# The column steps of two triangular inversions on GpSimd in place of VectorE, spread alike, with one more task step behind them

## The chip, the cores and the metric

The kernel runs on one core of one Trainium2 chip. The metric is the device time of that core in microseconds; the kernel before takes 983.41 us (median of 3 runs, 983.08 to 984.17). Engines are named as in the profile: PE is TensorE's matrix multiply, PEld its weight load, DVE is VectorE, ACT ScalarE, POOL GpSimd, SP SyncE. Each engine works off its own queue strictly in order; SP and POOL also issue the DMAs of their queues.

## The reference

One decoder block over 512 tokens of width 1024, in float32. A combined projection feeds two branches, a gated delta rule (8 heads, chunks of 64) and a forgetting attention (8 heads, causal softmax with a decay bias); they are merged by gates and followed by a squared-ReLU MLP. The part that the change touches is the triangular solve of the delta rule:

```
kk = jnp.einsum('bhncd,bhnsd->bhncs', k, k)
a_mat = jnp.where(tri_strict, beta[..., None] * kk * decay, 0.0)
rhs = jnp.concatenate([v * beta[..., None], k * (beta * jnp.exp(G))[..., None]], axis=-1)
sol = lax.linalg.triangular_solve(a_mat + eye, rhs, left_side=True, lower=True, unit_diagonal=True)
...
v_new = value_c - jnp.einsum('bhcd,bhde->bhce', kcum_c, s)
o = einsum(qdec_c, s) + einsum(attn_c, v_new);  s = s * dec_c + einsum(kdec_c, v_new)
...
m = sigmoid(gate_a) * y_a + sigmoid(gate_b) * y_b;  h = x + m @ w_out
x = h + jnp.square(jax.nn.relu(rmsnorm(h) @ w_up)) @ w_down
```

The kernel does not solve, it inverts the unit triangular matrices, here in blocks of 128 tokens, and multiplies by the inverse.

## The kernel before

**Stages.** The input is normalised and split into a rounded high part and a low rest; so is every weight (`hi` on ACT, line 256, and `lo` on DVE, line 257, a subtraction of two 128x1024 tiles in SBUF), and each product is three products on PE. First come the z gates and the projections of heads 0 to 3 (group 0), then six attention panels (`fox_pair`, products `fx`, lines 961 to 964), the projections of heads 4 to 7 (group 1), then the stream of 49 weight units (`stream`, products `st`, line 1011, 24 products each) for the rest of the attention heads and the gates, then the output projections and the MLP (`mlp`, line 1171), which holds PE from about 620 us to the end. Of every seven weight tiles of the stream four are not loaded but made from an earlier tile: POOL issues a DMA that adds onto the earlier raw tile (line 219), and it has to wait until that tile's `lo` was read out.

**Tasks.** Beside these loops run generator tasks, one per head, per inversion and scan, per attention worker. A call of `tick` advances each by one step, to its next `yield`. What a task writes between two yields is placed at that point of the program.

**What sets the order.** The program is written in that order, and a scheduler then rearranges each engine's queue by its own estimate of when each instruction is ready. So a change on one engine also moves rows of the others.

**The inversion** (`invert`, lines 659 to 747) runs once per group, over the 16 blocks of four heads at a time. The four 32x32 diagonal blocks of each are brought into one tile `E` (DVE transpose, line 669), and `X` starts as the identity. Then 31 columns are eliminated, two instructions each (lines 681 and 683): an outer product of a column of `E` with a row of `X` into `tmp`, and its subtraction from the rows below. The operands have r = 31 - j rows of n = j//2 + 1 elements per partition, 16 to 136 elements, 2,856 in all for each of the two lines. Each instruction reads what the one before it wrote. `INV_STEP` says after how much counted work the task yields. Behind the columns two DVE transposes make `Xd` (line 689) and its transpose `XT` (line 692), `X2` is filled (memset on POOL, copies on ACT), and PE joins the blocks by small products: `Qp` (line 707, needs `Xd`), `Tp` (line 720), `Q` and `T` (lines 739 and 741). After that `scan` goes over the four chunks.

**Around it on POOL**: scaling of queries and keys (`conv` line 652, `fqk` line 889), reciprocal roots by a power (`rsq`, line 346: `ssk`, `fss`, `sso`), the attention mask (`nd`, line 878), and the adding DMAs.

Of the kernel before, what the change touches and what calls it, by code (L numbers as in the profile page):

```python
# [10 lines left out]
ALU = mybir.AluOpType  # L11
# [4 lines left out]
P = 128  # L16
# [21 lines left out]
LA_NEW = 7  # L38
LA_RAW = 3
LA_SPLIT = 2  # L40
INV_STEP = (2500, 900)


def hybrid_block(tc, a, out):
# [21 lines left out]
    def nm(s):  # L66
        n_names[0] += 1
        return f"{s}_{n_names[0]}"
# [5 lines left out]
    def page(dt=F32, s="pg"):  # L74
        if s in FOX_TAGS:
            return fxp.tile([P, T], dt, tag=s, name=nm(s))
        tag = TAGS_OF.get(s, s)
        if tag in TAGS:
            return pgp.tile([P, T], dt, tag=tag, name=nm(s), bufs=TAGS[tag])
        return pgp.tile([P, T], dt, tag="pg", name=nm(s))  # L80
# [3 lines left out]
    def const(shape, s, dt=F32):  # L84
        return (cp if s in KEEP else cm).tile(shape, dt, tag=s, name=s)
# [15 lines left out]
    def atps(s="at"):  # L101
        return pat.tile([P, T], F32, tag="at", name=nm(s))

    def v3(ap, n):
        return ap.rearrange("p (a b) -> p a b", a=n)
# [8 lines left out]
    vec, act, pool = nc.vector, nc.scalar, nc.gpsimd  # L114
# [542 lines left out]
    x_id = const([P, B * HB], "x_id")  # L657

    def invert(AT, rest, ahead):

        bl = [slice(b * B, (b + 1) * B) for b in range(4)]
        dg = page(s="dg")
        for b in range(4):
            act.copy(v3(dg[bl[b], :], NI), AT[bl[b], :, bl[b]])
        yield
        E_ = sbp.tile([P, B * B], F32, tag="sub", name=nm("E"))
        vec.transpose(E_[:, :].rearrange("p (c d i) -> p c d i", c=B, d=2),
                      dg[:, :].rearrange("p (i c) -> p c i", i=NI).unsqueeze(2).to_broadcast([P, B, 2, NI]))  # L670
        X_ = page(s="X")
        vec.tensor_copy(X_, x_id)
        yield
        E3 = v3(E_[:, :], B)
        X3 = v3(X_[:, :], B)
        w = 0
        for j in range(B - 1):
            r, n = B - 1 - j, j // 2 + 1
            tmp = smp.tile([P, 144], F32, tag="tmp", name=nm("tmp"), bufs=2)
            t3 = tmp[:, 0:r * n].rearrange("p (a b) -> p a b", a=r)  # L680
            vec.tensor_tensor(t3, E3[:, j + 1:, j:j + 1].to_broadcast([P, r, n]),
                              X3[:, j:j + 1, 0:n].to_broadcast([P, r, n]), op=ALU.mult)
            vec.tensor_tensor(X3[:, j + 1:, 0:n], X3[:, j + 1:, 0:n], t3, op=ALU.subtract)
            w += 2 * (130 + r * n)
            if w > rest:
                w = 0
                yield
        Xd = page(s="Xd")
        vec.transpose(Xd[:, :].rearrange("p (i c d) -> p c d i", i=NI, d=2),
                      X_[:, :].rearrange("p (r c) -> p c r", c=HB))  # L690
        XT = page(s="XT")
        vec.transpose(XT, Xd)
        Xd3 = v3(Xd[:, :], NI)
        XT3 = v3(XT[:, :], NI)

        X2 = sbp.tile([P, NI, 64], F32, tag="sub", name=nm("X2"))
        pool.memset(X2[0:32, :, 32:64], 0.0)
        act.copy(X2[0:32, :, 0:32], Xd3[0:32, :, :])
        act.copy(X2[32:64, :, 32:64], Xd3[32:64, :, :])
        yield  # L700

        qs = page(s="Q")
        pqs = [atps("Qp") for _ in range(2)]
        for i in range(NI):
            for p in range(2):
                b0, b1 = bl[2 * p], bl[2 * p + 1]
                mm(pqs[p][b1, i * B:(i + 1) * B], AT[b0, i, b1], Xd3[b0, i, :], start=True, stop=True)
        for p in range(2):
            b1 = bl[2 * p + 1]
            (vec.tensor_copy if p else act.copy)(qs[b1, :], pqs[p][b1, :])  # L710
        for b in range(4):
            act.copy(AT[bl[b], :, bl[b]], XT3[bl[b], :, :])
        yield
        pqs = [atps("Tp") for _ in range(2)]
        pq = atps("Tq")
        for i in range(NI):
            s = slice(i * B, (i + 1) * B)
            for p in range(2):
                b0, b1 = bl[2 * p], bl[2 * p + 1]
                mm(pqs[p][b0, s], qs[b1, s], XT3[b1, i, :], start=True, stop=True)  # L720
                if p == 0:
                    mm(pq[b1, s], XT3[b1, i, :], qs[b1, s], start=True, stop=True)
        for p in range(2):
            b0, b1 = bl[2 * p], bl[2 * p + 1]
            act.mul(AT[b0, :, b1], v3(pqs[p][b0, :], NI), -1.0)
        vec.tensor_scalar(X2[bl[1], :, 0:32], v3(pq[bl[1], :], NI), -1.0, None, op0=ALU.mult)
        yield
        ahead()
        q6 = None
        for j0 in range(0, NI + 8, 8):  # L730
            last, more = q6, j0 < NI
            if last is not None:
                pt = atps("T6")
            if more:
                pq = atps("Q6")
            for i in range(8):
                s = slice(i * 64, (i + 1) * 64)
                if last is not None:
                    mm(pt[0:64, s], last[64:128, s], AT[64:128, j0 - 8 + i, 64:128], start=True, stop=True)
                if more:  # L740
                    mm(pq[64:128, s], AT[0:64, j0 + i, 64:128], X2[0:64, j0 + i, :], start=True, stop=True)
            if last is not None:
                act.mul(AT[0:64, j0 - 8:j0, 64:128], v3(pt[0:64, :], 8), -1.0)
            if more:
                q6 = page(s="Q6s")
                vec.tensor_copy(q6[64:128, :], pq[64:128, :])
            yield
# [4 lines left out]
    def fetch(g, hd, kind, c):  # L752

        t = page(s="hd")
        nc.sync.dma_start(v3(t[:, :], G), hd[kind, c])
        return [t[:, cs(i)] for i in range(G)]
# [74 lines left out]
    def group_chain(g, AT, hd, heads):  # L831
        while any(t in tasks for t in heads):
            yield
        got = []
        yield from invert(AT, INV_STEP[g], lambda: got.extend(fetch(g, hd, kind, 0) for kind in (3, 2, 4)))
        inverted[g] = True
        yield from scan(g, AT, hd, got)
# [385 lines left out]
    for n in range(KT):  # L1223
        s_, j, f = n // 4, n // 2 % 2, n % 2
# [165 lines left out]
    for k, (w, c, p, s_) in enumerate(MLP):  # L1390
# [6 lines left out]
        n = pos[0]  # L1397
# [122 lines left out]
```

## Time and profile before

| what | value |
|---|---|
| time, median of 3 runs | 983.41 us |
| span of the profiled execution | 980.2 us |
| granted PE clock | 1.000 |
| PE busy | 970.8 us (99%) |
| DVE busy | 710.9 us (73%) |
| ACT busy | 605.0 us (62%) |
| POOL busy | 240.2 us (25%) |
| column steps of group 0 on DVE | 143.49 to 170.44 us |
| column steps of group 1 on DVE | 354.41 to 400.06 us |
| first small product `Qp`, group 0 and 1 | 174.95 and 418.64 us |

Times within the trace count from the start of the span. A row of the timeline has the start, the duration, the engine, the line, the operation, what it writes and reads, the shapes, and the idle time before it with what ended it. "x4" merges four alike.

### The profile page before, as it was taken

The page shows a single profiled execution, that of the slowest core. Times are in us where ns is not written, and L with a number is a line of the kernel's source. Part 1 is how long each engine was busy: PE and PEld are TensorE (multiplying, and loading weights), DVE is VectorE, ACT ScalarE, POOL GpSimd, SP SyncE. Part 2 cuts the span into 40 slices and gives each one's busy share as a digit, 9 for nine tenths or more (in the row PEclk, how much of TensorE's full clock was granted, in tenths as well). Part 3 has the DMA queues.
Part 4 walks back from the last instruction along what each step waited for, and adds up shares of the span by engine and source line. Part 5 has one row for each costly group of instructions (what it writes and reads, how often), then busy time and mean ns, then how long its engine had stood idle before and what let it go on. Part 6 is the DMA issues. An engine that isn't in the chain of part 4 may idle for free.

```text
span 980.2 us, 17198 instructions
## 1 busy us (share of the span) xinstructions
PE 970.8 (99%) x6545; PEld 874.8 (89%) x6545; DVE 710.9 (73%) x1204; ACT 605.0 (62%) x1050; POOL 240.2 (25%) x236
## 2 busy tenths in 40 slices
PE   8999999999999999999999999999999999999998
PEld 6788899998888999999999888889989989988986
DVE  6877778566577789855656535889896697698596
ACT  7766444766564787867656422678755765666761
POOL 1544120202533513522320005312121121121110
PEclk9999999999999999999999999999999999999999
DMA  7647662475437885757887735688798888889884
GB/s 266 213 135 223 174 158 90 130 239 181 129 116 228 189 166 141 197 129 166 236 201 215 273 103 171 125 181 173 190 188 196 187 173 206 181 175 202 186 166 119
DMA packets 93442, 174.38 MB, mean 178 GB/s; under 512 B 8016, under 2 KB 49200, under 8 KB 93360
## 3 DMA queue, kind: packets, MB, share of 16 engines
q1 hardware_dynamic: 78928, 120.85, 38.8%
q0 software_dynamic: 14432, 52.44, 30.5%
q8 instruction: 51, 0.84, 0.4%
q14 instruction: 31, 0.25, 0.1%
HBM read 152.25 MB, written 21.02 MB: 177 GB/s over the span
## 4 chain that ended last, share of the span: by engine, by line
PE 92%; DVE 4%; DMA 2%; ACT 1%; issue 1%; SPq 0%; DVEq 0%
PE mlp L1171 36%; PE st L1011 12%; PE mm L279 8%; PE mm L276 8%; PE mm L275 8%; PE fx L964 2%; PE fx L961 2%; PE fx L962 2%; PE fo L944 2%; PE sc L919 1%; PE pT L935 1%; DVE lo L257 1%; PE kk L639 1%; PE kq L647 1%; DMA ux<-ud 1%; PE v L797 1%
## 5 line engine op out<-in xcount | busy, mean ns | idle before, releaser
L1402 ACT CAST hi<-draw 128x1024 fp32r<-128x1024 f32 x124 | 130.0, 1050 | 118.4 <-PE mlp L1171 100.4
L1409 DVE TENSOR_TENSOR lo<-draw,hi 128x1024 fp32r<-128x1024 f32 x124 | 151.3, 1222 | 44.8 <-ACT hi L1402 41.6
L256 ACT CAST hi<-raw 128x1024 fp32r<-128x1024 f32 (+1 forms) x62 | 62.9, 1021 | 82.6 <-PE mm L276 59.5
L1171 PE MATMUL mlp<-hi,shi 128*128 128x512 f32 x280 | 109.5, 391 | 0.1
L1171 PE MATMUL mlp<-hi,slo 128*128 128x512 f32 x280 | 109.1, 390 | 0.0
L1171 PE MATMUL mlp<-lo,shi 128*128 128x512 f32 x280 | 109.0, 389 | 0.0
L257 DVE TENSOR_TENSOR lo<-raw,hi 128x1024 fp32r<-128x1024 f32 (+1 forms) x62 | 73.9, 1197 | 29.1 <-ACT hi L256 13.4
L1171 PE MATMUL mlp<-shi,lo 128*128 128x256 f32 x448 | 90.3, 283 | 0.0
L1171 PE MATMUL mlp<-slo,hi 128*128 128x256 f32 x448 | 90.3, 283 | 0.0
L1171 PE MATMUL mlp<-shi,hi 128*128 128x256 f32 x448 | 90.3, 283 | 0.0
L276 PE MATMUL mm<-ulo,hi 128*128 128x512 f32 x216 | 85.0, 394 | 1.2 <-DVE ulo L290 1.2
L275 PE MATMUL mm<-uhi,hi 128*128 128x512 f32 x216 | 85.0, 395 | 0.0
L257 DVE TENSOR_TENSOR lo<-sraw,hi 128x1024 fp32r<-128x1024 f32 x49 | 60.7, 1240 | 20.9 <-ACT hi L256 20.1
L1171 PEld LDWEIGHTS mlp<-shi,hi 128*128 128x128 f32 x448 | 70.6, 192 | 0.9
L1171 PEld LDWEIGHTS mlp<-shi,lo 128*128 128x128 f32 x448 | 69.9, 192 | 0.0
L1171 PEld LDWEIGHTS mlp<-slo,hi 128*128 128x128 f32 x448 | 69.8, 192 | 0.0
L256 ACT CAST hi<-sraw 128x1024 fp32r<-128x1024 f32 x49 | 51.3, 1047 | 26.6 <-PE st L1011 16.2
L1171 PEld LDWEIGHTS mlp<-hi,shi 128*128 128x128 f32 x280 | 52.6, 188 | 11.1 <-issue 0.7
L1171 PEld LDWEIGHTS mlp<-lo,shi 128*128 128x128 f32 x280 | 52.6, 188 | 11.1
L1171 PEld LDWEIGHTS mlp<-hi,slo 128*128 128x128 f32 x280 | 52.6, 188 | 10.3
L219 POOL DMA_DIRECT2D draw<-w_d x30 | 26.3, 876 | 129.9 <-DVE lo L1409 120.8
L219 POOL DMA_DIRECT2D draw<-w_u x32 | 27.7, 866 | 122.6 <-DVE lo L1409 120.0
(336 smaller groups left out, 2466.6 us busy)
## 6 DMA issues: line engine op xcount, KB each, us to landing
draw<-w_u POOLq DMA_DIRECT2D x32, 512.0 KB, 5.7
draw<-w_d POOLq DMA_DIRECT2D x32, 512.0 KB, 6.5
sraw<-w_st POOLq DMA_DIRECT2D x28, 512.0 KB, 5.9
draw<-w_d SPq DMA_DIRECT2D x26, 512.0 KB, 4.4
raw<-w_gdn SPq DMA_DIRECT2D x24, 512.0 KB, 3.8
draw<-w_u SPq DMA_DIRECT2D x24, 512.0 KB, 4.4
sraw<-w_st SPq DMA_DIRECT2D x21, 512.0 KB, 5.5
hd<-hd SPq DMA_DIRECT2D x34, 256.0 KB, 5.4
```

What stands on the lines that cost most here:

```text
L219: nc.gpsimd.dma_start(raw, a[w][c, q, s_], accum_op=ALU.add)
L256: act.copy(hi[:, c], raw[:, c])
L257: vec.tensor_tensor(lo[:, c], raw[:, c], hi[:, c].bitcast(F32), op=ALU.subtract)
L275: mm(o, w, rhi(k), start=(k == 0), stop=False)
L276: mm(o, w, rlo(k), start=False, stop=False)
L279: mm(o, lo[:, k * cols:(k + 1) * cols], rhi(k), start=False, stop=(k == KT - 1))
L944: mm(po[:, cs(i)], vt[c], st[i][:, cs(c)], start=(c == 0), stop=(c == i))
L961: mm(o, uhi[k][:, cs(tb)], w, start=(k == 0), stop=False)
L1011: mm(o, u, w, start=first and t == 0 and k == 0 and j == 0 and x is hi, stop=x is lo and k == 3, skip_group_check=True)
L1171: return (lambda *args, **kw: tc.keep_in_program_order(f(*args, **kw))) if self.pinned[0] else f
L1402: pact.copy(hi, raws[m][0])
L1409: pvec.tensor_tensor(lo, raws[m][0], hi[:, :].bitcast(F32), op=ALU.subtract)
```

## The change

The 62 column instructions of each inversion are issued on POOL and no longer on DVE. The start value of `X` is copied by ACT and no longer by DVE. `INV_STEP` was 2500 for group 0 and 900 for group 1, which made 5 and 13 yields among the columns; it is 1600 for both, which makes 7 in each. One more `yield` stands behind the two transposes, ahead of `X2` and of the small products. Lines from 697 on move down by one.

```
-INV_STEP = (2500, 900)
+INV_STEP = (1600, 1600)
...
         X_ = page(s="X")
-        vec.tensor_copy(X_, x_id)
+        act.copy(X_, x_id)
         yield
...
-            vec.tensor_tensor(t3, E3[:, j + 1:, j:j + 1].to_broadcast([P, r, n]),
+            pool.tensor_tensor(t3, E3[:, j + 1:, j:j + 1].to_broadcast([P, r, n]),
                               X3[:, j:j + 1, 0:n].to_broadcast([P, r, n]), op=ALU.mult)
-            vec.tensor_tensor(X3[:, j + 1:, 0:n], X3[:, j + 1:, 0:n], t3, op=ALU.subtract)
+            pool.tensor_tensor(X3[:, j + 1:, 0:n], X3[:, j + 1:, 0:n], t3, op=ALU.subtract)
...
         XT3 = v3(XT[:, :], NI)
 
+        yield
         X2 = sbp.tile([P, NI, 64], F32, tag="sub", name=nm("X2"))
```

The first place is PE at the inversion of group 1. Before, `Qp` stands inside the 24th unit of the stream (its weights are `hi_4925` and `lo_4926`), behind the transposes of an attention head:

```order
L1011 MATMUL st_4340<-lo_4926,uhi_186 128x256
L1011 MATMUL st_4340<-hi_4925,uhi_183 128x256
L944 MATMUL fo_4817<-pTs_4752,fqk_3621 128x128
L898 MATMUL fqT_4851<-ident,fqk_3819 128x128
L899 MATMUL fkT_4852<-ident,fqk_3819 128x128
L898 MATMUL fqT_4851<-ident,fqk_3819 128x128
L899 MATMUL fkT_4852<-ident,fqk_3819 128x128
L898 MATMUL fqT_4851<-ident,fqk_4594 128x128
L899 MATMUL fkT_4852<-ident,fqk_4594 128x128
L898 MATMUL fqT_4851<-ident,fqk_4594 128x128
L899 MATMUL fkT_4852<-ident,fqk_4594 128x128
L707 MATMUL Qp_4866<-Xd_4793,AT_2910 32x32 x9
```

In the changed kernel it stands right behind the last product of the 18th unit (weights `hi_4640`, `lo_4641`):

```order
L945 MATMUL fo_4525<-pTs_4595,fqk_4233 128x128
L1012 MATMUL st_4373<-hi_4640,lo_2222 128x256 x2
L1012 MATMUL st_4373<-hi_4640,lo_2587 128x256 x2
L1012 MATMUL st_4373<-lo_4641,hi_2221 128x256 x2
L1012 MATMUL st_4373<-lo_4641,hi_2586 128x256 x2
L708 MATMUL Qp_4600<-Xd_4474,AT_2867 32x32
```

So PE comes to it six units of the stream earlier. In group 0 it moves a little the other way, further back among the products of an attention panel.

The second place is POOL in group 1. Before, the adding DMAs (`sraw<-w_st`) and the attention's rows stand there alone; now the columns stand between them, and each DMA is queued behind the columns written ahead of it. This is the end of the columns:

```order
L219 DMA sraw_4207<-w_st 128x1024
L681 TENSOR_TENSOR tmp_4414<-E_3973,X_3975 128x56
L683 TENSOR_TENSOR X_3975<-X_3975,tmp_4414 128x4x14
L681 TENSOR_TENSOR tmp_4417<-E_3973,X_3975 128x45
L346 TENSOR_TENSOR fss_4537<-fss_4537,expo 128x8
L683 TENSOR_TENSOR X_3975<-X_3975,tmp_4417 128x3x15
L890 TENSOR_TENSOR fqk_4298<-fqk_4298,fss_4537 128x512
L890 TENSOR_TENSOR fqk_4181<-fqk_4181,fss_4537 128x512
L681 TENSOR_TENSOR tmp_4420<-E_3973,X_3975 128x30
L219 DMA sraw_4644<-w_st 128x1024
L683 TENSOR_TENSOR X_3975<-X_3975,tmp_4420 128x2x15
L681 TENSOR_TENSOR tmp_4471<-E_3973,X_3975 128x16
```

From `E` to the last column POOL holds, in group 1, the 62 columns, seven adding DMAs, two `fss`, four `fqk` and one `nd`; in group 0 the 62 columns alone.

The third place is DVE in group 1, where `Xd` now waits for POOL. Behind it stand the next weight splits:

```order
L257 TENSOR_TENSOR lo_4755<-sraw_4644,hi_4754 128x1024
L932 RECIPROCAL fsm_4585<-fsm_4585 128x1
L933 TENSOR_SCALAR p_4586<-p_4586,fsm_4585 128x512
L257 TENSOR_TENSOR lo_4816<-sraw_4758,hi_4815 128x1024
L689 STREAM_TRANSPOSE Xd_4474<-X_3975 128x32x16
L692 STREAM_TRANSPOSE XT_4476<-Xd_4474 128x512
L711 COPY Q_4599<-Qp_4601 32x512
L257 TENSOR_TENSOR lo_4899<-sraw_4482,hi_4898 128x1024
L257 TENSOR_TENSOR lo_4963<-sraw_4644,hi_4962 128x1024
```

Between `E` and `Xd` DVE now holds 11 weight splits `lo` in group 1 and 4 in group 0, and no column.

## The prediction

> **What bounds the kernel now.** I read the page's busy line first, then its chain of waits.
>
> ```profile
> PE 970.8 (99%) x6545; PEld 874.8 (89%) x6545; DVE 710.9 (73%) x1204; ACT 605.0 (62%) x1050; POOL 240.2 (25%) x236
> PE 92%; DVE 4%; DMA 2%; ACT 1%; issue 1%; SPq 0%; DVEq 0%
> ```
>
> PE is the bound, and the change takes nothing off PE: it can only remove or add idle time there. Busy time by stretch shows how much there is around the two inversions (columns: the window, its length, then busy time and count of PE, PEld, DVE, ACT and POOL).
>
> ```profile
> 150.00:200.00 50.00, 49.52 (x578) 47.63 (x577) 35.56 (x91) 27.30 (x50) 5.47 (x5) 1.00 0.38 115
> 350.00:400.00 50.00, 49.83 (x396) 47.30 (x395) 47.14 (x126) 37.16 (x76) 15.31 (x16) 1.00 0.75 167
> 400.00:450.00 50.00, 50.00 (x563) 47.41 (x562) 31.43 (x62) 37.08 (x77) 16.23 (x15) 1.00 0.64 162
> 450.00:500.00 50.00, 49.80 (x419) 48.66 (x418) 30.09 (x75) 35.85 (x64) 14.86 (x14) 1.00 0.82 207
> ```
>
> PE idles 0.48 + 0.17 + 0 + 0.20 = 0.85 us in these 200 us. So the gain to be had is below 1 us, though DVE is nearly full at 350 to 400 (47.14 of 50). The chain of waits in order of time says what that does.
>
> ```profile
> 372.97 1.79 PE st L1011 x15
> 377.15 1.20 DVE lo L257
> 378.92 1.48 DVE X L683
> 396.72 0.97 DVE X L683
> 398.69 0.41 DVE p L932
> 399.14 0.66 PE pT L935 x4
> ```
>
> From 377 to 399 the chain does run over DVE, with the columns (`X`) between the weight splits, but PE has so much work queued that it loses 0.17 us. The first row also gives PE's pitch, 1.79 / 15 = 0.12 us per 256-wide product.
>
> **The change part by part.** *Taken off DVE:* 124 column instructions and two copies. What they cost on DVE is of no weight by itself: I take 0.4 us of PE's idle time as given back (half of the 0.85).
>
> *When PE comes to the small products.* It starts them here now, and these are the rows around the place that the changed order gives them in group 1.
>
> ```profile
> 174.95 1.20 PE L707 MATMUL Qp<-Xd,AT 32*32 32x32 f32 x64
> 396.65 0.64 PE L1011 MATMUL st<-hi,hi 128*128 128x256 f32 x4
> 418.64 1.66 PE L707 MATMUL Qp<-Xd,AT 32*32 32x32 f32 x64
> ```
>
> Counted over the two orders with the trace's pitch for each kind of row, PE's work ahead of `Qp` grows by 2.3 us in group 0 and shrinks by 20.9 us in group 1. So, with PE as full as now, it comes to them at 174.95 + 2.3 = 177.2 and at 418.64 - 20.9 = 397.7. The second row confirms this: the 19th unit starts there, and in the changed order `Qp` stands between the 18th and the 19th, with 0.7 us more of attention products ahead, which gives 397.3. I take 397.5.
>
> *When POOL has `X`.* The trace has no column on POOL, so I price one from its other rows.
>
> ```profile
> 142.08 2.28 POOL L889 TENSOR_TENSOR fqk<-fqk,fss 128x512 f32<-128x512 f32 x2
> 206.64 1.01 POOL L346 TENSOR_TENSOR sso<-sso,expo 128x4 f32<-128x4 f32 x1 [11.01 <-DVE sso L768]
> 269.62 1.28 POOL L583 TENSOR_TENSOR em<-em,upper 128x512 f32<-128x512 f32 x1 [4.85 <-ACT em L578]
> 315.69 1.64 POOL L346 TENSOR_TENSOR fss<-fss,expo 128x8 f32<-128x8 f32 x1 [1.97 <-DVE fss L885]
> 317.40 2.04 POOL L889 TENSOR_TENSOR fqk<-fqk,fss 128x512 f32<-128x512 f32 x2
> 330.64 0.88 POOL L219 DMA_DIRECT2D sraw<-w_st  x1 [1.82 <-DVE ssk L617]
> 331.24 1.33 POOL L346 TENSOR_TENSOR ssk<-ssk,expo 128x4 f32<-128x4 f32 x1
> 374.73 0.69 POOL L878 TENSOR_SCALAR_AFFINE_SELECT nd<-row 128x512 f32<-128x512 f32 x1
> 582.75 1.64 POOL L1229 TENSOR_TENSOR m<-gate,gate 128x256 f32<-128x256 f32 x1 [64.06 <-DVE gate L1227]
> ```
>
> The groups of L1229 (least, median and largest in ns):
>
> ```profile
> L1229 POOL TENSOR_TENSOR m<-gate,gate x16: 723/1407/1647, 582.7 to 622.4; 128x256 f32<-128x256 f32 x16
> ```
>
> 256 elements take 0.73 us (least of L1229), 512 take 1.28: 2.18 ns an element and 0.17 us fixed. With an operand spread from one column, as in the first of the two column lines, 512 take 1.02 (half of L889's 2.04): 1.7 ns. A row that reads the one before starts 0.07 us behind its end (315.69 + 1.64 to 317.40), and every column does. So a pair costs 2 x (0.17 + 0.07) us and 3.88 ns for each of its elements, an inversion 62 x 0.24 + 2,856 x 3.88 ns = 14.9 + 11.1 = **26.0 us**. Bounds: nothing fixed and no gap, 5,712 x 2.0 ns (1.02 / 512) = 11.4 us; or the fixed cost of the power (0.16 us an element between its 4 and 8, so 1.01 - 4 x 0.16 = 0.37 us), 62 x 0.44 + 5,712 x 2.18 ns = 39.7 us. I take 26.0, since L889 and L1229 are the same kind of instruction as the columns.
>
> *What holds POOL up.* L1229 takes 1.64 us and not 0.73 where it starts under a weight split:
>
> ```profile
> 582.58 1.22 DVE L257 TENSOR_TENSOR lo<-raw,hi 128x1024 fp32r<-128x1024 f32 x1
> 372.86 1.01 DVE L683 TENSOR_TENSOR X<-X,tmp 128x120 f32<-128x120 f32 x1
> ```
>
> L1229 came 0.17 us after `lo`, was 0.91 us late, and so waits for nearly all of `lo` (1.08 of 1.22). The second row is the reverse, a DVE column that took 1.01 us under the `fqk` of POOL. Less the 0.07 gap that is there anyway, I charge 1.0 us for each `lo` between `E` and `Xd`: 4.0 in group 0, 11.0 in group 1. Between nothing (each `lo` falls into a DMA or a wait) and 1.22 each lies all that I can bound.
>
> The Trainium skill ("SBUF — State Buffer", section "Who interferes with whom") calls this an exclusive lock: a DVE instruction with two SBUF inputs and a GpSimd one that reads SBUF block each other for a whole instruction, and `tensor_scalar` in a two-port mode does so too. The trace agrees on the first with the 0.91 us; no row here shows the second delaying POOL. By the rule the softmax scalings (L932, 9 of 0.42 us in group 1) would add up to 3.7 us more, and the sum below would come to 994.
>
> *Group 0.* The first row of POOL above ends at 142.08 + 2.28 = 144.36, and POOL has nothing else until `X` is done.
>
> ```profile
> 170.27 0.17 DVE L683 TENSOR_TENSOR X<-X,tmp 128x16 f32<-128x16 f32 x1
> 170.48 1.19 DVE L689 STREAM_TRANSPOSE Xd<-X 128x512 f32<-128x512 f32 x1
> 351.81 2.11 DVE L669 STREAM_TRANSPOSE E<-dg 128x1024 f32<-128x1024 f32 x1
> 399.89 0.17 DVE L683 TENSOR_TENSOR X<-X,tmp 128x16 f32<-128x16 f32 x1
> ```
>
> 144.36 + 26.0 + 4.0 = 174.4, with `Xd` (1.19) and two hand-overs 175.7, against 177.2 for PE: hidden, by 1.5 us, and 4 us later than DVE had it (170.44).
>
> *Group 1.* `E` is done at 351.81 + 2.11 = 353.9. Then POOL works off 26.0 of columns, 11.0 of waiting, 7 adding DMAs of 0.60 (330.64 to 331.24), two `fss` of 1.71, four `fqk` of 1.02 and one `nd` of 0.69: 26.0 + 11.0 + 4.2 + 3.4 + 4.1 + 0.7 = 49.4, so until 403.3, and `Xd` until 404.6. PE is there at 397.5 and stands **7.1 us**. DVE stands behind `Xd` too, with the next splits queued behind it, but these are for units that PE has not reached. The DMAs are late by as much as POOL. The one for the 18th unit stands behind 39 columns (39 x 0.24 + 3,950 x 1.94 ns = 17.0), three DMAs, one `fss`, two `fqk` and `nd` (6.2) and six `lo` (6.0), so it is issued at about 383.1. With the 5.9 us to landing of the page's list and the two casts of 1.1 and 1.2 us it is ready at about 391, and PE wants it 24 products and one attention product ahead of 397.5, at 394. It adds nothing of its own.
>
> ```profile
> sraw<-w_st POOLq DMA_DIRECT2D x28, 512.0 KB, 5.9
> ```
>
> ```profile
> 402.89 1.07 ACT L256 CAST hi<-sraw 128x1024 fp32r<-128x1024 f32 x1
> ```
>
> *The other edits.* `X` copied by ACT stands under the 2.1 us transpose of `E`; without that cover it would cost half of the cast above, 0.5 us, once per group. The new yield and the other `INV_STEP` act on the order alone, which is counted above; `X2`, which they push back, is needed only at `Q`, which stands behind `Qp` and `Tp`.
>
> *Sum* against the profiled execution: 980.2 + 7.1 - 0.4 = 986.9. The runs' median lies 983.41 - 980.2 = 3.2 above the span, so **990**.
>
> **Rivals.** (1) *The columns are cheap, and nothing changes.* It decides where POOL's work in group 1 shrinks by 7.1 us, at 26.0 - 7.1 = 18.9 us of columns or 0.30 us for one instead of 0.42, or with only four of eleven `lo` in the way. DVE's own price speaks for it:
>
> ```profile
> L681 DVE TENSOR_TENSOR tmp<-E,X x62: 174/262/1020, 143.5 to 399.7; 128x126 f32<-128x126 f32 x6, 128x30 f32<-128x30 f32 x4, 128x56 f32<-128x56 f32 x4, 128x78 f32<-128x78 f32 x4
> ```
>
> With 0.26 us and no port to wait for, POOL would be done in time: 983. Against it stands that no POOL row with 256 elements takes below 0.72. (2) *Faster.* DVE loses its columns, so weight splits and softmax come earlier, and PE's 0.85 us of idle time and some stretched products at 372 to 475 go: 981. It needs rival 1 and more than the idle time that the windows show. (3) *Dear columns.* At the power's fixed cost (39.7 us) group 1 is 13.7 us later still, and group 0, with only 1.5 us to spare, stands 12.2 us: 980.2 + 20.8 + 12.2 - 0.4 + 3.2 = 1016; at a third of the way, 30.6 us, 4.6 and 3.1 more, 998.
>
> The Trainium skill ("GPSIMD Engine Reference", section "Engine selection") gives two-input elementwise work to VectorE, GpSimd being about twice as slow. By that the columns would take 62 x 0.26 x 2 = 32 us, and the time would be about 1001. No row of this trace has POOL at the columns' sizes, so none shows it.
>
> **How the numbers follow.** Forecast, PE stands a few us at `Qp` of group 1: 0.55, range of its own 985.6 to 997. Rival 1: 0.23, 983. Rival 2: 0.10, 981. Rival 3: 0.12, 998 and more. A difference below 0.2% (2 us) can't be told from no change. Slower is the forecast and rival 3, 0.67; same is rival 1, 0.23; faster rival 2, 0.10. The range 982 to 1000 leaves out most of rival 2 and the upper half of rival 3.
>
> **What would show it.** Right: POOL rows for L681 and L683 of about 0.35 us at a pitch of 0.42, some of 1.3 to 1.5 where a `lo` runs; the last one near 403 in group 1; PE idle before `Qp` (now L708) for about 7 us, put down to DVE's `Xd`, and no such gap in group 0. Wrong: `Xd` of group 1 done before 397, or a pitch below 0.30; PE's wait at the 18th unit's weights and not at `Qp`; or the loss somewhere else, as at the attention's rows behind `fss`.

## The result and the profile after

The changed kernel takes **1008.24 us** (median of 4 runs, 1004.48 to 1010.12) against 983.25 us of the kernel before in the same comparison: ratio **1.0247**, 95% interval 1.0223 to 1.0271. The forecast was 990 us with a range of 982 to 1000: the direction was right, the size was not. The profiled execution's span grew from 980.2 to 1006.5 us, by 26.3 us where the sum had 6.7.

The page's busy line and its chain by engine:

```profile
PE 979.5 (97%) x6545; PEld 881.4 (88%) x6545; DVE 683.5 (68%) x1078; ACT 600.9 (60%) x1048; POOL 293.3 (29%) x360
PE 80%; POOL 6%; DVE 5%; issue 3%; ACT 3%; DMA 2%; SPq 0%; POOLq 0%; DVEq 0%; ACTq 0%
```

PE is busy for 9 us longer with the same 6545 products, and the span is 26 us longer; PE's part of the chain fell from 92 to 80%, and POOL, which had none, has 6%. Two kinds of loss are in that: PE stands idle, and PE is slower while it works. The view of the cores shows the second:

```profile
core 0: 1006.5 us, clock 0.987
```

Before, the granted clock was 1.000. The four executions of the changed kernel spanned from 1002.8 us at a granted clock of 0.993 to 1008.4 us at 0.986, so the second kind of loss differs by some us from one execution to the next, and what follows is read from one of them. Where both happen is read from the windows (length, busy time and count of PE, PEld, DVE, ACT and POOL, granted clock, DMA share, GB/s), of the changed kernel first and then of the kernel before:

```profile
175.00:200.00 25.00, 23.07 (x343) 21.78 (x343) 17.53 (x28) 15.18 (x27) 5.99 (x8) 0.93 0.30 90
275.00:300.00 25.00, 20.04 (x103) 16.57 (x103) 15.28 (x28) 13.23 (x30) 9.38 (x8) 0.97 0.47 131
300.00:325.00 25.00, 21.82 (x89) 17.61 (x89) 15.74 (x28) 9.44 (x26) 6.59 (x5) 0.77 0.45 125
400.00:425.00 25.00, 18.50 (x189) 17.29 (x188) 13.83 (x29) 13.12 (x27) 19.62 (x35) 0.92 0.71 138
```

```profile
275.00:300.00 25.00, 25.00 (x132) 21.10 (x131) 18.69 (x36) 13.73 (x41) 8.30 (x7) 1.00 0.51 146
300.00:325.00 25.00, 25.00 (x131) 21.09 (x130) 21.20 (x43) 11.48 (x30) 9.17 (x8) 1.00 0.73 203
```

The largest loss lies in the projections of heads 4 to 7, between the two inversions, where no column runs: 103 and 89 products in 25 us instead of 132 and 131, DVE far from full, and the clock down to 0.77. What PE waited for, from the view of waits (total, times, longest):

```profile
PE mm L275 <- DVE conv L599: 8.1, 3, 4.3
PE fo L945 <- ACT pTs L938: 4.9, 2, 3.0
PE Qp L708 <- DVE Xd L689: 3.5, 1, 3.5
PE mm L275 <- ACT gate L992: 1.4, 1, 1.4
```

To put sizes to the places I compared the distance from each PE instruction's start to the next one's with the median distance behind the same line and shape in the kernel before, and added up the differences (a shorter distance counts as negative). That gives 11.5 us over the span before and 37.5 after, 26.0 more:

| stretch of the span | PE idle, before and after | all loss, before and after | more |
|---|---|---|---|
| 150 to 250 (group 0's small products) | 0.5, 1.9 | 1.1, 4.3 | 3.2 |
| 250 to 350 (projections of group 1) | 0.0, 8.1 | 0.6, 14.6 | **14.0** |
| 350 to 500 (stream, inversion of group 1) | 0.4, 6.5 | 2.8, 9.7 | 6.9 |
| 500 to 620 | 0.0, 1.4 | -0.1, 1.6 | 1.7 |
| the rest | 3.6, 3.8 | 7.1, 7.2 | 0.1 |

17.2 us of the 26.0 are idle time; the other 8.8 are products that ran longer. In the chain of waits these stand directly behind the long stretches of idle time:

```profile
299.70 0.76 PE mm L275
300.47 0.43 PE mm L276
...
304.73 0.43 PE mm L276
...
305.42 0.23 PE mm L276
```

For 5 us a 512-wide product takes 0.43 us and not 0.23; the window 300 to 305 has a granted clock of 0.50.

**POOL itself.** The two column lines (least, median, largest in ns), and two columns beside the pair of weight splits that they meet (the first row is DVE's):

```profile
L681 POOL TENSOR_TENSOR tmp<-E,X x62: 216/397/1502, 144.4 to 419.9; 128x126 f32<-128x126 f32 x6, 128x30 f32<-128x30 f32 x4, 128x56 f32<-128x56 f32 x4, 128x78 f32<-128x78 f32 x4
L683 POOL TENSOR_TENSOR X<-X,tmp x62: 221/411/1454, 144.7 to 420.2; 128x126 f32<-128x126 f32 x6, 128x30 f32<-128x30 f32 x4, 128x56 f32<-128x56 f32 x4, 128x78 f32<-128x78 f32 x4
```

```profile
149.30 2.56 DVE L257 TENSOR_TENSOR lo<-raw,hi 128x1024 fp32r<-128x1024 f32 x2 [5.95 <-ACT fq L903]
149.33 1.45 POOL L683 TENSOR_TENSOR X<-X,tmp 128x100 f32<-128x100 f32 x1
150.86 1.21 POOL L681 TENSOR_TENSOR tmp<-E,X 128x96 f32<-128x96 f32 x1
```

Group 0's columns last from 144.41 to 175.78 (31.4 us; 30.0 had been worked out), group 1's from 371.42 to 420.45 (49.0; 49.4 had been).

**Who is late at 300 us.** The chain of waits of the changed kernel up to the long wait:

```profile
291.61 1.28 ACT L578
292.91 0.60 ACT em L578
293.50 0.58 ACT conv L596
...
295.04 0.86 DVE AT L641 x3
295.90 1.31 DVE conv L599 x2
...
297.38 0.86 DVE am L650 x3
298.25 1.32 DVE conv L599 x2
...
299.70 0.76 PE mm L275
```

`em` is the exponential in the decay factors of group 1's heads (`decays`, a task that the kernel starts when group 0's task has ended), and the 1.28 us ahead of it are a table load. Behind it on ACT stands the first of the four convolution rows of a projection; behind that one DVE has to do `AT`, `conv`, `am`, `conv` in this order (`AT` and `am` are a head's key and query products times the decay factors); and PE gets an accumulator back only from the last `conv`. This `em` is the last of four. Before, the last one ran at 272.80.

**Who is late at 409 us.** POOL, ACT and DVE of the changed kernel around the two waits of group 1:

```profile
401.21 0.92 POOL L219 DMA_DIRECT2D sraw<-w_st  x1
...
407.69 1.04 ACT L256 CAST hi<-sraw 128x1024 fp32r<-128x1024 f32 x1 [4.19 <-DMA sraw<-w_st]
408.65 0.26 ACT L938 COPY pTs<-pT 128x128 f32<-128x128 f32 x1
...
420.48 1.08 DVE L689 STREAM_TRANSPOSE Xd<-X 128x512 f32<-128x512 f32 x1 [4.08 <-POOL X L683]
```

An adding DMA stands on POOL between the columns. It is issued at 401.2 and has landed at 407.6; ACT has stood 4.19 us at the cast of that tile, and queued behind the cast is `pTs`, which PE wants for `fo` (the longest `fo` wait, 3.0 us, ends at 408.96). After it PE runs on to `Qp` and waits 3.5 us for `Xd`.

### The profile page after: what moved, and what is told of

Read it like the earlier page. It is cut to its first block, busy times and chain, and to the rows that moved or that the text cites. A ratio compares the mean times of both kernels' runs of the same rounds, so it can differ in the third digit from the quotient of the medians.

```text
span 1006.5 us, 17194 instructions
## 1 busy us (share of the span) xinstructions
PE 979.5 (97%) x6545; PEld 881.4 (88%) x6545; DVE 683.5 (68%) x1078; ACT 600.9 (60%) x1048; POOL 293.3 (29%) x360
## 4 chain that ended last, share of the span: by engine, by line
PE 80%; POOL 6%; DVE 5%; issue 3%; ACT 3%; DMA 2%; SPq 0%; POOLq 0%; DVEq 0%; ACTq 0%
PE mlp L1172 35%; PE st L1012 9%; PE mm L275 7%; PE mm L276 7%; PE mm L279 7%; POOL tmp L681 2%; POOL X L683 2%; PE fx L965 1%; PE fx L963 1%; PE fx L962 1%; PE fo L945 1%; DMA row<-oad 1%; PE sc L920 1%; DVE conv L599 1%; PE o L819 1%
## 5 line engine op out<-in xcount | busy, mean ns | idle before, releaser
L275 PE MATMUL mm<-uhi,hi 128*128 128x512 f32 x216 | 88.8, 413 | 8.1 <-DVE conv L599 8.1
L276 PE MATMUL mm<-ulo,hi 128*128 128x512 f32 x216 | 88.1, 409 | 1.2 <-DVE ulo L290 1.2
L257 DVE TENSOR_TENSOR lo<-sraw,hi 128x1024 fp32r<-128x1024 f32 x49 | 61.3, 1251 | 37.5 <-ACT hi L256 31.8
L219 POOL DMA_DIRECT2D draw<-w_d x30 | 26.3, 876 | 130.4 <-DVE lo L1410 120.7
```

What stands on the lines that cost most here:

```text
L219: nc.gpsimd.dma_start(raw, a[w][c, q, s_], accum_op=ALU.add)
L257: vec.tensor_tensor(lo[:, c], raw[:, c], hi[:, c].bitcast(F32), op=ALU.subtract)
L275: mm(o, w, rhi(k), start=(k == 0), stop=False)
L276: mm(o, w, rlo(k), start=False, stop=False)
```

## The experiments

Two theories of the loss between 250 and 350 us stand against each other at first. S: it comes from group 0's task steps, eight from the first column to the small products instead of five, through everything that waits for group 0's end. P: it comes from the columns on POOL, by their length or by the lock with DVE.

All times are medians, each against the kernel before on the same chip. Line numbers in the experiments' rows are up to six higher than in the kernel before. In the code `rest` is the group's step size from `INV_STEP`. "The loss at 250 to 350" is worked out as in the table above, from the one profiled execution of each kernel.

**1. The steps without the engine.** The changed kernel with the columns back on DVE.

```
-            pool.tensor_tensor(t3, E3[:, j + 1:, j:j + 1]...)
+            vec.tensor_tensor(t3, E3[:, j + 1:, j:j + 1]...)
-            pool.tensor_tensor(X3[:, j + 1:, 0:n], X3[:, j + 1:, 0:n], t3, op=ALU.subtract)
+            vec.tensor_tensor(X3[:, j + 1:, 0:n], X3[:, j + 1:, 0:n], t3, op=ALU.subtract)
```

> All of the change but the engine: the 62 column instructions go back to VectorE, while the even step size (1600, 1600), the added task step and the copy of X on ScalarE stay. Theory S (steps): group 0 now has 8 task steps from the first column to the small products instead of 5, so everything that waits for group 0's end, the decay factors of group 1's heads above all, is written later, and the projections at 275 to 330 us run short. Then about 14 us of the 25 stay: 983 + 14 = 997 us (993 to 1001), with PE waits of 3 to 5 us before conv rows near 300 and 320 us. Theory P (the columns on GpSimd, by their length or by the lock with VectorE): those gaps go with the columns, 983 to 986 us.

989.93 us against 982.26, ratio 1.0076 (1.0052 to 1.0100). PE's waits:

```profile
PE mm L275 <- DVE conv L599: 5.4, 2, 3.2
PE Qp L708 <- DVE Xd L689: 1.9, 1, 1.9
```

With no column on POOL the waits for `conv` are there, at 292.8 and 312.0 us, and so is a wait at `Qp`, since group 1's fewer steps bring PE to it earlier. Theory P falls for this part. But it is 7.7 us and not the 14 that theory S gave: the loss at 250 to 350 is 9.3 us here and 14.6 in the changed kernel.

**2. The engine without the steps.** The kernel before with those two lines on `pool`, and nothing else.

> The kernel before with the 62 column instructions on GpSimd and nothing else: step sizes (2500, 900), no added task step, X copied on VectorE. Theory S: no gap at 275 to 330 us; the small products of group 1 stand 20 us of PE work later than in the changed kernel, behind the 49 us of columns, so there is no wait there either: 983 to 988 us. Theory P: the gaps at 300 and 320 us stay, 997 to 1008 us.

990.69 us, ratio 1.0086 (1.0058 to 1.0114), above the range of theory S and below that of theory P. The loss at 250 to 350 is 0.7 us, as theory S says; but there are waits at `fqT` (2.5 us at 380 us, for POOL's `fqk`), at `Tp` of group 0 (2.0 us) and at `Qp` of group 0 (0.5 us). Engine and steps alone cost 8.4 and 7.7 us; together they cost 25.0, so some 9 us come only from both.

**3. Group 0's steps undone in the changed kernel.**

```
-INV_STEP = (1600, 1600)
+INV_STEP = (2500, 1600)
...
-        yield
+        if rest < 2000:
+            yield
         X2 = sbp.tile(...)
```

> The changed kernel, with group 0's task steps as before (step size 2500, no added step there); group 1 keeps 1600 and the added step. Theory S: the decay factors are written where they were (249 of PE's work instead of 255), the losses at 275 to 330 us (14 us) go, those in group 1 (waits of 3 us at the attention and 3.5 us at Qp, and the slow clock behind them) stay: 1008 - 14 = 994 us (990 to 998). Theory P: 1005 to 1008 us.

995.04 us, as expected (994): 13.2 us less than the changed kernel, and the loss at 250 to 350 is 0.7 us. Group 0's three more task steps are the cause of the largest part.

**4. The decay factors let go earlier in the changed kernel.**

```
+    near = []
...
-        while after is not None and after in tasks:
+        while after is not None and after in tasks and not near:
             yield
...
         for c in range(NCH):      # scan
+            if c == NCH - 1:
+                near.append(g)
```

> The changed kernel, with one thing else: the decay factors of group 1 are let go at the start of the last chunk of group 0's scan, three task steps ahead of its end, instead of at its end. Theory S: their products stand at 239 of PE's work (255 in the changed kernel, 247 before), the gaps at 300 and 320 us go, and the time is about 994 us (990 to 999). Theory P, or any theory in which not the decay factors but something else of group 0 is late: 1004 to 1010 us.

996.39 us, 11.9 less. The last `em` runs at 273.9 instead of 292.9 us, the loss at 250 to 350 is 3.3 us. So that loss goes through the decay factors, though group 0 keeps its late end. PE now reaches `Qp` of group 1 earlier and gives a part back there:

```profile
PE Qp L710 <- DVE Xd L691: 5.3, 1, 5.3
PE fo L949 <- ACT pTs L942: 4.3, 2, 2.4
PE mm L275 <- DVE conv L601: 2.4, 2, 2.2
```

**5. One step, and two.** The kernel before with the added step in group 0 alone, and with group 0's step size alone (two steps more).

```
+        if rest > 2000:
+            yield
         X2 = sbp.tile(...)
```

> The kernel before with one thing else: the added task step of the change, in group 0 alone (columns on VectorE, step sizes 2500 and 900). The decay factors' products come at 254, 262 and 266 of PE's work instead of 247, 256 and 261, the block products kk stay at 270. Theory S1 (the loss at 275 to 330 us grows with every step): about a third of the 8.7 us that all three steps cost on VectorE, 986 us. Theory S2 (a threshold: only where kk itself moves back, 275 instead of 270, do the projections run short): no change, 982 to 984 us.

982.80 us, ratio 1.0005 (0.9995 to 1.0014).

```
-INV_STEP = (2500, 900)
+INV_STEP = (1600, 900)
```

> The kernel before with one thing else: the step size of group 0 is 1600 instead of 2500, which makes two more task steps there. The decay factors' products come at 255, 262 and 266 of PE's work, kk at 273 instead of 270. Theory S1: two thirds of 8.7 us, about 989 us, with PE waits for conv rows near 290 and 310 us. Theory S2: between no change and that, 983 to 987 us, with at most one such wait.

983.12 us, ratio 1.0007 (0.9997 to 1.0016). Each has one wait for `conv` (0.9 and 0.4 us) and a loss at 250 to 350 of 1.7 and 1.2 us. Theory S1, a price for each step, falls.

**6. All three steps in group 0**, both edits of experiment 5 in the kernel before (with group 0's step size at 1600 the condition reads `rest > 1000`).

> The kernel before with all three more task steps of the change in group 0 (step size 1600 and the added step), group 1 as before, columns on VectorE. One step and two steps alone made no difference (982.8 and 983.1). Theory S2: kk is at 275 now and the threshold is passed, 988 to 991 us with the two waits near 292 and 312 us. Theory S1, by which the loss grows evenly from step to step, would give 984 at most after these two runs.

990.27 us, ratio 1.0087 (1.0059 to 1.0115), with the same two waits for `conv` as in experiment 1, 5.4 us in all. Two steps cost nothing that can be measured, three cost 8 us: the projections had slack, and the third step uses it up. (2.4 us of this profile's loss lie at the start of the program, outside of the change.)

**7. Late decay factors alone.** The kernel before with the decay factors let go three, and in a second run five, task steps after group 0's end.

```
         while after is not None and after in tasks:
             yield
+        for _ in range(3 * g):
+            yield
```

> The kernel before, with its inversions untouched; only the decay factors of group 1 are let go three task steps after group 0's end instead of at it. Block products kk come at 275 of PE's work and kq at 280, as in the run with all the change's steps on VectorE (before: 270 and 274). Theory S2 (late decay factors alone make the loss): PE waits of 2 to 4 us for conv rows near 290 and 310 us and a lower granted clock behind them, 988 to 992 us. If the inversion's or the scan's own later place makes the loss, 982 to 984 us.

982.09 us, ratio 0.9993 (0.9982 to 1.0004). Theory S2 in this form falls: `kk` and `kq` stand where they stand in experiment 1, and nothing is lost.

> The kernel before, inversions untouched, the decay factors of group 1 let go five task steps after group 0's end (three made no difference: 982.1, its last exponential em on ScalarE at 283.4 us, against 287.1 to 292.9 us in the runs that lose). The D products come at 255, 270 and 276 of PE's work, kk at 281. Theory S3 (the loss begins where the last em comes behind about 285 us, whatever put it there): em near 288, a PE wait of 2 to 4 us near 295 us, 986 to 992 us. Theory R (group 0's later scan, with its copies and sums on ScalarE and VectorE among the projections, is needed as well): 982 to 984 us.

991.12 us, ratio 1.0092 (1.0069 to 1.0114), within what theory S3 gave, but not at its place:

```profile
PE st L1013 <- DVE conv L601: 7.1, 1, 7.1
```

It is one wait at 332 us, at the end of the projections, where one of 2 to 4 us near 295 us was expected. Late decay factors are enough to make a loss of this size. The two waits of the changed kernel need more, and that group 0's later scan is the rest is argued from the runs, not shown.

**8. The steps with early decay factors**, the edit of experiment 4 in the kernel of experiment 1.

> All the change's steps, columns on VectorE, as in the run that took 989.9, with the decay factors let go three task steps ahead of group 0's end. The scan of group 0 stays as late as in that run. Theory S3: the waits near 292 and 312 us go (their part of the loss was 9 us), that at Qp of group 1 (2.0 us) stays: 983 to 985 us. Theory R, by the scan's rows: 987 to 990 us.

986.21 us, ratio 1.0045 (1.0026 to 1.0063), between the two theories. The loss at 250 to 350 falls from 9.3 to 2.5 us and the wait of 1.9 us at `Qp` stays, as S3 says; the profile has 3.7 us more at 530 us (a wait for a gate's row, with a lower clock behind it) and 2.5 us at the start, whose cause I did not follow. The set of positions is then this (the last `em`, the loss at 250 to 350, and PE's idle time in it):

| kernel | last `em` starts | loss at 250 to 350 | of it PE idle |
|---|---|---|---|
| before | 272.8 | 0.6 | 0.0 |
| changed, decay factors early | 273.9 | 3.3 | 2.4 |
| one step more | 274.8 | 1.7 | 0.9 |
| all steps on DVE, decay factors early | 277.0 | 2.5 | 1.6 |
| two steps more | 280.5 | 1.2 | 0.4 |
| decay factors 3 steps late | 283.4 | 0.9 | 0.2 |
| decay factors 5 steps late | 286.8 | 9.5 | 7.1 |
| all steps on DVE | 287.1 | 9.3 | 5.4 |
| three steps more | 289.8 | 6.3 | 5.4 |
| changed | 292.9 | 14.6 | 8.1 |

That three steps more lose less than all steps on DVE does not come from PE's waits: the idle time is the same 5.4 us, but the granted clock in the 5 us behind the two waits was 1.00 and 1.00 in the one execution, 0.66 and 0.72 in the other.

**9. One group at a time on POOL**, in the kernel before.

```
+            eng = pool if rest > 2000 else vec
-            vec.tensor_tensor(t3, ...)
+            eng.tensor_tensor(t3, ...)
...
```

The subtraction is changed in the same way; this picks group 0, and for group 1 the condition reads `rest < 2000`.

> The kernel before with the columns of group 0 alone on GpSimd. From the run with both groups there: Xd comes at 178.8 us instead of 171.7, ScalarE then has six copies to do ahead of Q, so the small products Tp wait 2 us and Qp 0.7 us; with the baseline's 0.9 us of loss there taken off, +2.5 us: 985 us (984 to 987). If group 1's queue on GpSimd is the whole loss of that run, 983 us.

987.50 us, ratio 1.0059 (1.0044 to 1.0074), 2.5 us above the expectation. The waits are those expected (`Tp` 2.0 us, `Qp` 0.5); what was missed is the clock behind them, 3.1 us here and 0.3 in experiment 2 behind a wait of the same length. Up to the end of that wait PE does the same rows at nearly the same times in both runs; from 183 to 188 us these are the windows of experiment 2 and of this run:

```profile
183.00:188.00 5.00, 4.79 (x121) 4.44 (x122) 1.77 (x5) 4.90 (x12) 0.00 (x0) 1.00 0.32 100
183.00:188.00 5.00, 4.84 (x104) 4.07 (x105) 1.77 (x5) 4.90 (x12) 0.00 (x0) 0.52 0.32 102
```

So the price behind a wait differs between two executions that do the same up to there (they ran on two chips).

> The kernel before with the columns of group 1 alone on GpSimd. From the run with both groups there: the keys' and queries' scaling fqk stands behind columns on GpSimd, the transposes fqT wait 2.5 us at 380 us and the products run 1.7 us longer at a lower granted clock behind that: +4 to +5 us, 987 us (985 to 989). If group 0's late X is the whole loss, 983 us.

987.27 us, ratio 1.0048 (1.0031 to 1.0065), as expected; but PE, which group 0 does not delay here, comes sooner to `fqT` and waits longer. POOL's rows there, and the wait:

```profile
376.23 1.66 POOL L346 TENSOR_TENSOR fss<-fss,expo 128x8 f32<-128x8 f32 x1
...
378.30 2.03 POOL L890 TENSOR_TENSOR fqk<-fqk,fss 128x512 f32<-128x512 f32 x2
```

```profile
PE fqT L899 <- POOL fqk L890: 4.6, 1, 4.6
```

Ahead of `fss` and between it and `fqk` stand columns on POOL. So with group 1's old step size it is the attention's rows that are late, not `Qp`.

**10. Where group 0's part comes from.** The kernel of `pool_group0`, with the four copies of `XT` into `AT` on DVE in group 0.

```
-            act.copy(AT[bl[b], :, bl[b]], XT3[bl[b], :, :])
+            (vec.tensor_copy if rest > 2000 else act.copy)(AT[bl[b], :, bl[b]], XT3[bl[b], :, :])
```

> The run with the columns of group 0 alone on GpSimd (987.5), with one thing else: in group 0 the four copies of XT into AT, which stand on ScalarE between Xd and the copy of Q, are made by VectorE. Theory: X late by 7 us costs there because six copies of 0.62 us on ScalarE stand ahead of Q. Then Q comes about 2.5 us sooner, the wait of Tp (2.1 us) goes and the low clock behind it (up to 3.1 us) with it, the 0.7 us at Qp stays: 983 to 984.5 us. If the lateness of Xd itself is the cost: 986 to 988 us.

984.01 us, ratio 1.0018 (1.0008 to 1.0029), as expected. ACT's rows without and with the edit:

```profile
178.75 0.62 ACT L699 COPY X<-Xd 32x512 f32<-32x512 f32 x1 [5.64 <-DVE Xd L690]
...
180.00 2.50 ACT L713 COPY AT<-XT 32x512 f32<-32x512 f32 x4
182.53 0.58 ACT L711 COPY Q<-Qp 32x512 f32<-32x512 f32 x1
```

```profile
179.81 0.58 ACT L711 COPY Q<-Qp 32x512 f32<-32x512 f32 x1
```

`Xd` comes within 0.2 us of the same time, `Q` is copied 2.7 us sooner, the wait of `Tp` shrinks from 2.0 to 0.3 us, and 3.5 us of time go with it. What a late `X` costs in group 0 is ACT's queue behind it.

**11. Group 1's steps undone in the changed kernel.**

```
-INV_STEP = (1600, 1600)
+INV_STEP = (1600, 900)
...
-        yield
+        if rest > 1000:
+            yield
```

> The changed kernel with group 1's task steps as before (step size 900, no added step there), group 0 as in the change. The small products of group 1 stand at 402 of PE's work instead of 388. Theory: the loss at 275 to 330 us (14 us) stays; at 375 to 430 us the waits at Qp (3.5) and at fo (3.0) and the clock behind them (2.1) go, and no more than 2 us come back at the attention's fqk, which stands behind columns: 1008 - 9 + 1 = 1000 us (996 to 1003). If group 1's steps are of no account: 1006 to 1009 us.

1002.04 us, 6.2 less than the changed kernel where 8 were expected. The loss at 250 to 350 stays (13.8), of the waits in group 1 that at `Qp` is nearly gone (0.6 us in two pieces, from 3.5), but that at `fo` is still there (2.5 us at 408 us), against the expectation.

**12. The three remedies together**: experiments 4, 10 and 11 in the changed kernel, with all columns on POOL.

> The changed kernel, columns of both groups on GpSimd and group 0's three more task steps kept, with the three remedies of the runs before together: the decay factors let go at the start of group 0's last chunk, group 0's copies into AT on VectorE, group 1's task steps as before (900, no added step). If the parts add up: 1008.2 less 11.9 (decay factors), 3.5 (copies) and 6.2 (group 1's steps) is 986.6 us (984 to 989), and what stays is the attention's wait behind the columns of group 1, near 400 us. If they hang on each other, above 990 us.

990.00 us, ratio 1.0077 (1.0057 to 1.0097), 3.4 above the sum of the parts. 18 of the 25 us are gone. PE's waits:

```profile
PE fo L950 <- ACT pTs L943: 4.0, 2, 2.6
PE mm L275 <- DVE conv L601: 1.6, 2, 1.1
```

No version with the columns on POOL reached the kernel before; the nearest is experiment 10, with group 0 alone.

**13. What an idle stretch of PE costs.** A tail behind the last product of the kernel before: blocks of 36 products, each fed through a chain that starts at the block before (so its time is longer by the tail; one run). In words, not in the kernel's code:

```
+    for k in (0, 4, 1, 5, 2, 6, 3, 8, 0, 1, 2, 3, 4, 5):
+        36 products into one accumulator, input x0
+        k VectorE copies, one after the other
+        x0 = ScalarE copy of the last one
+    36 products more
```

> The kernel before with a tail behind its last product: 15 blocks of 36 products of 128x512, each block's input made from the result of the block before by a chain of 0 to 8 VectorE copies and one on ScalarE, so that PE stands idle for known times between blocks (about 1 to 7 us). It measures what an idle stretch costs besides itself. Theory C1 (the granted clock falls behind idle stretches above a bound near 3 us): blocks behind shorter ones take 36 x 0.227 = 8.2 us, behind longer ones about 11 us. Theory C2 (it depends on more than the length of the last stretch, since after waits of 2.0 and 2.2 us in the runs so far the products took 1.8 to 3.1 us longer, and after one of 2.9 us only 0.1): blocks behind stretches of 2 to 3 us fall on both sides.

The timeline of PE (start, length of the block, and in brackets the idle time ahead of it):

```profile
996.89 10.05 PE L1443 MATMUL tail<-tx,tw 128*128 128x512 f32 x36 [2.83 <-ACT tx L1450]
...
1056.79 8.46 PE L1443 MATMUL tail<-tx,tw 128*128 128x512 f32 x36 [2.37 <-ACT tx L1450]
1069.92 9.80 PE L1443 MATMUL tail<-tx,tw 128*128 128x512 f32 x36 [4.67 <-ACT tx L1450]
```

Eight blocks behind 0.69 to 2.37 us took 8.45 to 8.49 us, six behind 2.83 to 4.67 us took 9.80 to 10.10. Here theory C1 holds: up to 2.4 us a stretch costs little more than itself (the block that had no stretch ahead of it took 8.32), from 2.8 us on another 1.35 to 1.65 us, whatever its length.

## Why the prediction was wrong, step by step

- **PE is the bound, and less than 1 us is to be had.** Right. DVE was freed of 27 us of busy time (710.9 to 683.5), and no run shows a gain from it.
- **The price of a column, 0.42 us.** Right within a tenth. The least durations of the 62 rows of an inversion add up to 22.5 us (for the one shape that always met a split I took its neighbour's), with 62 hand-overs of 0.078 us 27.3 us: 0.44 us a column, 27.3 and not 26.0 us an inversion. POOL's nearest rows gave the price, and rival 1 (below 0.30) is out. DVE's median was 0.262 us, POOL's are 0.397 and 0.411, 1.5 times that. The Trainium skill ("GPSIMD Engine Reference", section "Engine selection") makes it about two.
- **Each weight split holds POOL up by 1.0 us.** Right in group 0, a little dear in group 1: above the least durations the columns took 4.1 us more in group 0 (four splits) and 9.0 in group 1 (eleven, of which some met a DMA or `fss` instead of a column). The Trainium skill ("SBUF — State Buffer", section "Who interferes with whom") would add `tensor_scalar` in a two-port mode. On POOL this hardly shows: of 13 columns that overlap the softmax's scaling (L933) and no split, ten were at most 0.01 us longer than the least of their shape, three 0.08, 0.18 and 0.35: 0.65 us in all, and not the 3.7 of that reading. It may show on DVE: the one 128x128 scaling beside a column took 0.47 us, the seven others 0.28 to 0.29.
- **Group 0: hidden, by 1.5 us.** Wrong in what it looked at. `Qp` did not wait, as said. But the cover was counted for PE alone, and the first to wait for `Xd` is ACT: six copies of 0.62 us stand behind it and ahead of what PE wants next. In the changed kernel the chain of waits runs from these copies over `Q`, a cast, rows on DVE (`lo`, two `ux`) and another cast to `pTs` (the rows below), and PE waits 1.9 us at 188 us for `pTs`, with the clock at 0.66 in the 5 us behind it (the windows at the end): 3.2 us more than before. Experiment 10 shows the mechanism, in the old order.

```profile
178.88 0.62 ACT AT L713
...
182.75 0.58 ACT Q L711
...
187.49 0.50 ACT pTs L938
```

- **Group 1: PE stands 7.1 us.** Right in size, in two pieces. `E` comes 17.4 us later than before, and PE had lost 17.4 us more than before by then (0.2 up to 150 us, 3.2 and 14.0), so the race between POOL and PE was the one that was worked out. That POOL's 49.0 us come so near to 49.4 is in part luck: the columns took 1.3 us more than reckoned, the waits for splits 2.0 less. PE waited 2.95 us at `fo` and 3.55 us at `Qp`, 6.5 together, and not 7.1 at `Qp`.
- **The DMA adds nothing of its own.** Wrong: the `fo` wait is exactly the DMA queued behind the columns. I followed the tile to PE, which did not want it yet, and not to ACT, where its cast blocks the attention's copies. By these times it took from `Qp`'s wait what it cost and did not add to the sum; this is argued, and in experiment 11 the `fo` wait stays where `Qp`'s has nearly gone.
- **The new yield and the other step size "act on the order alone, which is counted above".** This is the step that failed. What had been counted of the order was PE's place at `Qp`. Not counted was that group 0 ends three task steps later, that the decay factors of group 1's heads start only at that end, and that their exponentials then stand on ACT among the convolution rows of the projections: 14.0 us of the 26. Experiment 3 takes it away (0.7 us left), 4 most of it (3.3 left), 6 makes part of it on DVE; how much of it the engine adds (9.3 with DVE, 14.6 with POOL, of it 5.4 and 8.1 idle) is measured in 1, not explained.
- **Idle time costs its length.** This stood behind every term, and is not so: 8.8 of the 26 us are products that ran longer, most of them at a lower clock behind a wait. This part is that of one execution.
- The 1.7 us at 553 us (a wait for a gate's row) was not expected either. It comes and goes over the runs without a pattern that I could name, and stays open.

In the terms of the sum: 7.1 measured 6.5; idle time of 1.9 us (group 0), 8.1 (projections) and 1.4 (gate's row) was missing, and 8.8 of slower products. That is 26.7 us; PE's idle time of before in these stretches (0.9) goes off, 0.2 elsewhere come on: 26.0. That the loss might lie "somewhere else, as at the attention's rows behind `fss`" had been named as the sign of a wrong prediction; it is what experiment 9 shows with the old step size, and `fo` in the changed kernel.

## What to carry to other kernels

Where a program's order comes from task steps, a step added in one task has to be followed to every task that starts at its end, and there to the engine that hands PE's accumulators back: two steps cost nothing here and the third 8 us. Whoever moves work to an engine with slack must ask who stands in the queue behind each late result, on ACT and DVE as much as on PE. A lower clock behind a wait of PE can add to it, about half as much again in this profile (8.8 us on 17.2), but not behind every wait, and not alike in every execution.

## What the runs showed of the hardware that was not expected

Behind an idle stretch the granted clock of PE can fall to 0.50 for a few us (300 to 305 us, and 320 to 325): 512-wide products take 0.43 us. In the tail of experiment 13 the bound lies between 2.37 and 2.83 us of idle time, and the price is the same 1.35 to 1.65 us for all above it. The Trainium skill ("TensorE: Matmul & The Clock Gate", section "Why this matters for your kernels") says that idle gaps above about 3 us put the clock back to half; the half agrees with the 0.50, and the bound in the tail is a little lower. Within the kernel the length of the last stretch does not decide: 1.92 us at 188 us were followed by a clock of 0.66 over 5 us, and 2.95 us at 409 us by 1.00, in the windows of the changed kernel (the second row is the stretch behind 300 us):

```profile
188.00:193.00 5.00, 4.97 (x30) 4.83 (x30) 1.47 (x3) 2.24 (x4) 0.17 (x1) 0.66 0.16 56
...
300.00:305.00 5.00, 5.00 (x13) 3.83 (x13) 1.35 (x2) 2.06 (x3) 0.00 (x0) 0.50 0.57 174
...
409.00:415.00 6.00, 6.00 (x46) 5.52 (x47) 5.62 (x13) 4.89 (x10) 5.54 (x9) 1.00 0.83 133
```

And a wait of 3.18 us has a clock of 0.50 behind it in the changed kernel (320 us), of 0.72 in experiment 1 and of 1.00 in experiment 6 (313 us), as that of 1.98 us has 1.00 and 0.52 in experiments 2 and 9, behind the same rows. What decides there was not tried.
